# Early norm inputs, squares on other engines, a narrower index-key weight and a wider table row in a hybrid decoder layer

## The chip, the cores and the metric

The kernel runs on one core of one Trainium2 chip. The metric is device time in microseconds (us) of one execution; lower is better. An execution's time is a little longer than the span of its trace, which runs from the first to the last instruction.

Five engines work side by side, each through its own list of instructions in order: PE (TensorE; PE rows are matmuls, PEld rows are their weight loads), DVE (VectorE), ACT (ScalarE), POOL (GpSimd) and SP (SyncE, which issues most DMAs). They wait for each other by semaphores.

## The reference

One decoder layer over 256 tokens of 1024 features. What bears on the change is cut out here:

```python
def rms_norm(x, g):
    xf = x.astype(jnp.float32)
    y = xf * lax.rsqrt(jnp.mean(xf * xf, axis=-1, keepdims=True) + EPS)
    return (y * g.astype(jnp.float32)).astype(x.dtype)
...
def token_mixer(xn, w_in, conv_w, conv_b, w_r, b_r, w_i, b_i, lam, w_pa, w_pb, w_pc, w_o, rel_bias):
    proj = xn @ w_in
    (qa, ka, va, qb, kb, vb, qi, ki, wi, xc, yc, gates) = jnp.split(proj, IN_OFFSETS, axis=-1)
    y_a = moba_attention(..., rel_bias[:, :N_HEADS_A])
    y_b = dsa_attention(..., ki, wi, rel_bias[:, N_HEADS_A:])
    y_c = rg_lru(causal_depthwise_conv(xc, ...), ...) * jax.nn.gelu(yc)
    merged = g[:, :, 0] * (y_a @ w_pa) + g[:, :, 1] * (y_b @ w_pb) + g[:, :, 2] * (y_c @ w_pc)
    return merged @ w_o
...
    x = x + token_mixer(rms_norm(x, norm_mix_g[l]), ...)
    x = x + squared_relu_mlp(rms_norm(x, norm_mlp_g[l]), ...)
    return rms_norm(x, final_norm_g)
```

`ki` (64 columns) and `wi` (8 columns) are the index keys and index weights of the sparse branch. In both attention branches the logit of query t and key s gets a bias `rel_bias[bucket(t - s), head]`, 16 heads in all.

## The kernel before

Every product is kept near float32 accuracy by splitting each operand into a high part (a rounded copy, made by ACT) and a low part (the rest, made by DVE with one subtraction), and by three matmul passes: high by high, high by low, low by high. A weight tile is two halves of 128 x 1024 floats. A half arrives by DMA in a `raw` buffer (5 of them), ACT writes its `hi` (L133) and DVE its `lo` (L134); there are 6 `hi` and 6 `lo` buffers. PE then spends 24 matmuls of 256 columns on a half (L198). A `raw` buffer is free, and SP may issue the next load into it, once its `lo` is done.

The first stage is written out by hand (`manual_schedule`: on ACT, DVE, POOL and PE its instructions stand in the order of the code). The transposed input arrives in four slices of 128 x 512 in `xr`, each with a quarter of weight tile 0 behind it. For a slice ACT writes two pieces of `xnh` (L291), DVE two of `xnl` (L293), then both split the weight slice, and PE runs 12 matmuls into `ps_qi0` (L300). The norm's scale 1/rms is left out at this point and multiplied in later. It comes from squares of the slices (`sq`, L307 on POOL, L309 on ACT for the last), three sums (L311) and a fold (`sqs`, L312) on POOL, a ones-matmul over partitions (`ps_r`, L316), `v` (L322, DVE), the power -1/2 (`y`, L323, POOL), four small DVE instructions (L325 to L328, giving `r1`) and two diagonal matrices (`dg`, L332), which PE spreads over all partitions (L340). PE meanwhile runs weight tile 1 (second half of the index queries, `ps_qi1`), the index keys and weights (`ps_kw`, L336) and the next tiles. `first_queries` (L274 to L278) turns `ps_qi0` and `ps_qi1` into operands; it is one ACT and five DVE instructions.

POOL also runs a chain of some 20 instructions of four columns (L462 to L474) for the recurrence's decay, each waiting for the last.

PSUM for projections is three accumulators (`acc_tile`). `ps_qi0`, `ps_xc0` and `ps_yc0` lie in the same one, in the built programs of before and after; `ps_yc0` can start when DVE has read `ps_xc0` (`xp`, L398).

The bias: a table of 33 x 16 numbers times a one-hot matrix gives 16 rows of 384 (`psr`, L371), DVE copies them to `rrow` (L373), and one DMA from POOL's queue (L375) writes each row 32 times to DRAM (`toep`), 512 runs of 383 floats. Eight loads of each attention branch read from there (L383). DVE adds the first of these at L587.

After the first stage a scheduler that works on the code's priorities sets the order on each engine; `order` rows below show what came out.

Of the kernel before, what the change touches and what calls it, by code (L numbers as in the profile page):

```python
# [20 lines left out]
F32 = mybir.dt.float32  # L21
# [17 lines left out]
NB = 383  # L39
TOEP_W = 384  # L40
COPIES = 32
TOEP_H = COPIES * 386


C_GMIX, C_GMLP, C_CW, C_CB, C_BR, C_BI, C_LAM = 0, 8, 16, 32, 36, 40, 44
# [13 lines left out]
def layer(ctx, tc, x, xf, wts, kiwi, small, wri, rel_bias, onehot, gfin, out):  # L59
# [16 lines left out]
    def f(ap):  # L76
        return ap.bitcast(F32)
# [136 lines left out]
    xnl = const.tile([P, 8, S], F32R, name="xnl", tag="xnl")  # L214
    xn = (xnh, xnl)

    xr = [wp.tile([P, 1024], F32, tag="raw", name=f"xr{j}", bufs=RAW_BUFS) for j in range(2)]
    w0 = [tuple(wp.tile([P, 1024], dt, tag=p, name=f"{p}0_{j}", bufs=n)
                for p, dt, n in (("raw", F32, RAW_BUFS), ("hi", F32R, HL_BUFS), ("lo", F32R, HL_BUFS)))
          for j in range(2)]  # L220
# [2 lines left out]
        nc.sync.dma_start(xr[i // 2][:, d], xf[:, s])  # L223
        nc.sync.dma_start(w0[i // 2][0][:, d], wts[0, :, s])
    loaded[1] = load(1)
    kw = big("kw")
    nc.sync.dma_start(kw, kiwi)
    loaded[2] = load(2)
    next_tile[0] = 2
# [50 lines left out]
    def split_tile(i, j):  # L280
        raw, hi, lo = loaded[i][j]
        split(hi, lo, raw)

    with tc.manual_schedule(engines=ENGINES):
        pv = ps_q[0].rearrange("p (c t) -> p c t", c=2)
        for i in range(4):
            xi = xr[i // 2].rearrange("p (k t) -> p k t", k=4)
            d = slice(i % 2 * 512, (i % 2 + 1) * 512)
            raw, hi, lo = (z[:, d] for z in w0[i // 2])
            for k in (2 * i, 2 * i + 1):  # L290
                nc.scalar.activation(xnh[:, k, :], xi[:, k % 4, :], AF.Copy, scale=sp[:, C_GMIX + k:C_GMIX + k + 1])  # L291
            for k in (2 * i, 2 * i + 1):
                nc.vector.scalar_tensor_tensor(xnl[:, k, :], xi[:, k % 4, :], sp[:, C_GMIX + k:C_GMIX + k + 1],  # L293
                                               f(xnh[:, k, :]), op0=ALU.mult, op1=ALU.subtract)
            split(hi, lo, raw)
            for n, (a, b) in enumerate(((0, 0), (0, 1), (1, 0))):
                for k in (2 * i, 2 * i + 1):
                    ww = w0[i // 2][1 + a].rearrange("p (k c) -> p k c", k=4)
                    for c in range(2):
                        nc.tensor.matmul(pv[:, c, :], ww[:, k % 4, c * P:(c + 1) * P], xn[b][:, k, :],  # L300
                                         start=(i == 0 and n == 0 and k == 0 and c == 0),
                                         stop=(i == 3 and n == 2 and k == 7 and c == 1))

        for i in range(4):
            xi = xr[i // 2][:, i % 2 * 512:(i % 2 + 1) * 512]
            if i < 3:
                nc.gpsimd.tensor_mul(sq[i], xi, xi)  # L307
            else:
                nc.scalar.activation(sq[i], xi, AF.Square)  # L309
            if i > 0:  # L310
                nc.gpsimd.tensor_add(sq[0], sq[0], sq[i])  # L311
        nc.gpsimd.tensor_add(sqs, sq[0][:, :S], sq[0][:, S:])  # L312
        split_tile(1, 0)
        fmajor(ps_q[1], [z[1:] for z in loaded[1]], xn, cs=(0,))
        for t in range(2):
            nc.tensor.matmul(ps_r[:, S + t:S + t + 1], sqs[:, t * P:(t + 1) * P], ones[:, :1], start=True, stop=True)  # L316
        split_tile(1, 1)
        fmajor(ps_q[1], [z[1:] for z in loaded[1]], xn, cs=(1,))
        first_queries(0)

        v, y, b = (sm.tile([P, 2], F32, name=f"{n}_n1", tag=n) for n in ("v", "y", "b"))
        nc.vector.tensor_scalar(v, ps_r[:, S:S + 2], 1.0 / DM, EPS, op0=ALU.mult, op1=ALU.add)  # L322
        nc.gpsimd.tensor_tensor(y, v, mhalf.to_broadcast([P, 2]), op=ALU.pow)  # L323
        split(kwh, kwl, kw.rearrange("p (k c) -> p k c", c=P))
        nc.vector.tensor_mul(b, y, y)  # L325
        nc.vector.tensor_mul(b, b, v)
        nc.vector.tensor_scalar(b, b, -0.5, 1.5, op0=ALU.mult, op1=ALU.add)
# [37 lines left out]
    psr = att_tile("psr", "t")  # L365
    ohr = tmp("ohr", 384, F32R)[:33]
    nc.scalar.activation(ohr, oh, AF.Copy)
    tabs = [tiny_.tile([33, 16], F32R, name=f"tab{p}") for p in "hl"]
    split(*tabs, tab)
    for m in range(2):  # L370
        nc.tensor.matmul(psr[:16, :384], tabs[m], ohr, start=(m == 0), stop=(m == 1))  # L371
    rrow = tmp("rrow", 384)[:16]
    nc.vector.tensor_copy(rrow, psr[:16, :384])  # L373
    toep = dpool.tile([16, TOEP_H], F32, name="toep")
    nc.gpsimd.dma_start(  # L375
        bass.AP(tensor=toep.tensor, offset=toep.offset, ap=[[TOEP_H, 16], [TOEP_W + 1, COPIES], [1, NB]]),
        rrow[:, None, :NB].to_broadcast([16, COPIES, NB]))

    def load_bias(h0, name):

# [573 lines left out]
```

## Time and profile before

| | before |
|---|---|
| median of 3 runs | 457.63 us (457.39 to 457.86) |
| the profiled execution | 457.67 us |
| its span | 455.9 us |
| PE busy | 443.4 us (97%) |
| DVE busy | 341.4 us (75%) |
| ACT busy | 264.7 us (58%) |
| POOL busy | 30.9 us (7%) |
| mean granted TensorE clock | 0.997 of full speed |

The page's slices (40 of them, 11.4 us each, a digit is the busy share in tenths) show where each engine works:

```profile
PE   6899899999999999999999999999999999999994
DVE  7979899999989999975788686655555555555545
ACT  6467668775459698675634457444444444444463
POOL 6920110000010100000000000000000000000000
DMA  7869967524765453555555654556555555565202
```

The busy share of an engine is an average over stages with different limits; a stage is read from its own rows. Two rows of a timeline, a start and a later start on the same engine, give the time between them. PE's busy time includes the draining of its pipeline, so that a gap is longer between the weight loads (PEld) than PE's own idle time says.

### The profile page before, as it was taken

The numbers are of one execution on the slowest core, as the hardware profiler recorded it, in microseconds if no ns is written. First come the engines' busy times: TensorE is split into PE (matmuls) and PEld (weight loads), VectorE is DVE, ScalarE is ACT, GpSimd is POOL, SyncE is SP. The second block draws the span as 40 slices with busy tenths as digits, with TensorE's granted clock in tenths as the row PEclk, the third lists the DMA queues.
The fourth block names the chain that finished last, engine by engine and source line by source line (L and its number), as shares of the span: only waits on it lengthen the run. The fifth ranks groups of instructions, "written<-read, shape, count | busy, mean of one in ns | idle before, by whom it ended". The sixth has DMA issues, their size and how long they took to land.

```text
span 455.9 us, 7378 instructions
## 1 busy us (share of the span) xinstructions
PE 443.4 (97%) x2738; PEld 398.6 (87%) x2738; DVE 341.4 (75%) x652; ACT 264.7 (58%) x439; POOL 30.9 (7%) x66
## 2 busy tenths in 40 slices
PE   6899899999999999999999999999999999999994
PEld 6899889989988888888888889999999999999984
DVE  7979899999989999975788686655555555555545
ACT  6467668775459698675634457444444444444463
POOL 6920110000010100000000000000000000000000
PEclk9999999999999999999999999999999999999998
DMA  7869967524765453555555654556555555565202
GB/s 261 280 241 216 316 221 237 197 95 136 252 211 187 136 185 98 185 185 184 182 170 188 223 163 149 184 192 191 188 189 191 188 188 186 190 191 185 88 0 93
DMA packets 23840, 83.65 MB, mean 184 GB/s; under 512 B 2987, under 2 KB 3020, under 8 KB 23804
## 3 DMA queue, kind: packets, MB, share of 16 engines
q1 hardware_dynamic: 22700, 80.28, 53.4%
q0 software_dynamic: 960, 2.88, 3.0%
q8 instruction: 21, 0.34, 0.3%
q14 instruction: 15, 0.12, 0.1%
q10 hardware_dynamic: 144, 0.02, 0.0%
HBM read 81.34 MB, written 1.83 MB: 182 GB/s over the span
## 4 chain that ended last, share of the span: by engine, by line
PE 88%; DMA 3%; DVE 3%; POOL 3%; issue 2%; ACT 1%; SPq 0%; DVEq 0%; ACTq 0%
PE ps_up L198 20%; PE pd L775 19%; PE ps_g L208 14%; PE ps_p L208 7%; PE po L208 5%; DMA raw<-wts 3%; PE ps_qa L198 3%; PE ps_qb L198 3%; PE ps_kb L198 3%; PE ps_ka L198 3%; PE ps_vb L208 2%; PE ps_va L208 2%; DVE lo L134 1%; PE ps_yc L198 1%; POOL sp L468 1%
## 5 line engine op out<-in xcount | busy, mean ns | idle before, releaser
L134 DVE TENSOR_TENSOR lo<-raw,hi 128x1024 fp32r<-128x1024 f32 (+1 forms) x146 | 178.8, 1236 | 81.5 <-ACT hi L133 81.0
L133 ACT ACTIVATE hi<-raw 128x1024 fp32r<-128x1024 f32 (+1 forms) x146 | 150.0, 1044 | 123.8 <-PE pd L775 42.8
L775 PE MATMUL pd<-hi,hh 128*128 128x512 f32 (+1 forms) x128 | 49.4, 387 | 0.0
L775 PE MATMUL pd<-hi,hl 128*128 128x512 f32 (+1 forms) x128 | 49.4, 387 | 0.0
L775 PE MATMUL pd<-lo,hh 128*128 128x512 f32 (+1 forms) x128 | 49.2, 386 | 0.0
L198 PE MATMUL ps_up<-x2h,hi 128*128 128x256 f32 x256 | 36.6, 283 | 0.0
L198 PE MATMUL ps_up<-x2h,lo 128*128 128x256 f32 x256 | 36.6, 283 | 0.0
L198 PE MATMUL ps_up<-x2l,hi 128*128 128x256 f32 x256 | 36.6, 283 | 0.0
L198 PEld LDWEIGHTS ps_up<-x2h,hi 128*128 128x128 f32 x256 | 34.0, 191 | 1.0
L198 PEld LDWEIGHTS ps_up<-x2h,lo 128*128 128x128 f32 x256 | 33.3, 192 | 0.0
L198 PEld LDWEIGHTS ps_up<-x2l,hi 128*128 128x128 f32 x256 | 33.3, 192 | 0.0
L208 PE MATMUL ps_g<-hi,xnh 128*128 128x512 f32 x96 | 30.4, 391 | 0.0
L208 PE MATMUL ps_g<-lo,xnh 128*128 128x512 f32 x96 | 30.3, 393 | 0.0
L208 PE MATMUL ps_g<-hi,xnl 128*128 128x512 f32 x96 | 30.2, 392 | 0.0
L775 PEld LDWEIGHTS pd<-lo,hh 128*128 128x128 f32 x128 | 24.0, 188 | 4.9
L775 PEld LDWEIGHTS pd<-hi,hh 128*128 128x128 f32 x128 | 24.1, 188 | 4.5
L775 PEld LDWEIGHTS pd<-hi,hl 128*128 128x128 f32 x128 | 24.1, 188 | 4.4
L208 PEld LDWEIGHTS ps_g<-hi,xnh 128*128 128x128 f32 x96 | 17.9, 188 | 3.4
L208 PEld LDWEIGHTS ps_g<-lo,xnh 128*128 128x128 f32 x96 | 17.8, 188 | 3.6
L208 PEld LDWEIGHTS ps_g<-hi,xnl 128*128 128x128 f32 x96 | 17.8, 188 | 3.4
L167 POOL TENSOR_TENSOR ssq_n<-q_n 128x1 f32<-128x1 f32 x2 | 0.4, 194 | 279.4 <-ACT scr_n L165 279.4
L663 ACT ACTIVATE g<-ps_g,rh 128x512 f32<-128x512 f32 x12 | 8.2, 682 | 9.4 <-PE ps_g L208 9.4
(370 smaller groups left out, 823.0 us busy)
## 6 DMA issues: line engine op xcount, KB each, us to landing
raw<-wts SPq DMA_DIRECT2D x142, 512.0 KB, 4.9
xr<-xf SPq DMA_DIRECT2D x4, 256.0 KB, 6.2
raw<-wts SPq DMA_DIRECT2D x4, 256.0 KB, 5.8
x<-x SPq DMA_DIRECT2D x2, 512.0 KB, 4.1
biasb<-toep POOLq DMA_DIRECT2D x8, 128.0 KB, 7.0
biasa<-toep POOLq DMA_DIRECT2D x8, 128.0 KB, 2.8
out<-o SPq DMA_DIRECT2D x2, 512.0 KB, 2.6
toep<-rrow POOLq DMA_DIRECT2D x1, 766.0 KB, 10.3
```

The source lines that it names most:

```text
L133: nc.scalar.activation(hi, raw, AF.Copy)
L134: nc.vector.tensor_sub(lo, raw, f(hi))
L167: nc.gpsimd.tensor_add(ssq, q[:, 0:1], q[:, 1:2])
L198: nc.tensor.matmul(pv[:, c, :], ww[a][:, k, :], xx[b][:, k, :], start=(n == 0 and k == 0 and (c == 0 or not part)), stop=(n == 2 and k == ...
L208: nc.tensor.matmul(ps, xx[b][:, k0 + k, d], ww[a][:, k, :], start=(first and n == 0 and k == 0), stop=(last and n == 2 and k == nk - 1))
L468: nc.gpsimd.tensor_mul(sp8, sp8, sq_)
L663: nc.scalar.activation(g[:, t, :], ps, AF.Tanh, scale=rh[:, t:t + 1])
L775: nc.tensor.matmul(ps, hid[g][b][:, c, d], w_down[g][c][a][:, s], start=(g == (NG - LAG if o else 0) and c == 0 and m == 0), stop=(g == NG ...
```

## The change

Four edits are made together.

- The transposed input's slices land in the two tiles `xt` that later hold the token-major x, and not in two `raw` buffers. All five `raw` buffers are then free for weights. Weight tile 1's second half is now loaded ahead of `kw`.
- All four squares are on ACT, behind the `hi` of both halves of tile 1. The three sums and the fold are on DVE. The ones-matmul stands behind both halves of tile 1, not between them. `v` is read, and POOL's power asked for, ahead of `first_queries(0)`.
- `kiwi` is loaded without its 56 zero columns (288 KB for 512 KB), split as 8 x 72 columns, and POOL sets the remaining columns of `kwh` and `kwl` to zero. The spreading of `dg` stands behind all of `ps_kw`.
- The bias table has each head's column 8 times, so that `psr` and `rrow` have 128 rows, and the DMA to `toep` takes 4 copies from each of 128 partitions, not 32 from each of 16. The number of runs and of bytes stays.

```diff
--- before.py
+++ after.py
@@ -27,6 +27,7 @@
 DRAM = bass.MemoryType.DRAM
 
 P = 128
+KW = 72
 S = 256
 DM = 1024
 NH = 8
@@ -39,7 +40,7 @@
 NB = 383
 TOEP_W = 384
 COPIES = 32
-TOEP_H = COPIES * 386
+TOEP_H = COPIES * (TOEP_W + 1)
 
 
 C_GMIX, C_GMLP, C_CW, C_CB, C_BR, C_BI, C_LAM = 0, 8, 16, 32, 36, 40, 44
@@ -214,7 +215,8 @@
     xnl = const.tile([P, 8, S], F32R, name="xnl", tag="xnl")
     xn = (xnh, xnl)
 
-    xr = [wp.tile([P, 1024], F32, tag="raw", name=f"xr{j}", bufs=RAW_BUFS) for j in range(2)]
+
+    xr = xt
     w0 = [tuple(wp.tile([P, 1024], dt, tag=p, name=f"{p}0_{j}", bufs=n)
                 for p, dt, n in (("raw", F32, RAW_BUFS), ("hi", F32R, HL_BUFS), ("lo", F32R, HL_BUFS)))
           for j in range(2)]
@@ -223,7 +225,7 @@
         nc.sync.dma_start(xr[i // 2][:, d], xf[:, s])
         nc.sync.dma_start(w0[i // 2][0][:, d], wts[0, :, s])
     loaded[1] = load(1)
-    kw = big("kw")
+    kw = big("kw")[:, :8 * KW]
     nc.sync.dma_start(kw, kiwi)
     loaded[2] = load(2)
     next_tile[0] = 2
@@ -260,6 +262,8 @@
     qiq = big("qiq", F32R).rearrange("p (c j t) -> p c j t", c=4, j=2)
     qil = tmp("qil", 512, F32R).rearrange("p (c t) -> p c t", c=4)
     kwh, kwl = (z.rearrange("p (k c) -> p k c", c=P) for z in (big("kwh", F32R), big("kwl", F32R)))
+    for z in (kwh, kwl):
+        nc.gpsimd.memset(f(z[:, :, KW:]), 0.0)
     rr = const.tile([P, S], F32, name="rr")
     r1 = tiny_.tile([P, 2], F32, name="r1")
     ki2 = tmp("ki2", S)
@@ -300,28 +304,24 @@
                         nc.tensor.matmul(pv[:, c, :], ww[:, k % 4, c * P:(c + 1) * P], xn[b][:, k, :],
                                          start=(i == 0 and n == 0 and k == 0 and c == 0),
                                          stop=(i == 3 and n == 2 and k == 7 and c == 1))
+        split_tile(1, 0)
+        split_tile(1, 1)
 
         for i in range(4):
-            xi = xr[i // 2][:, i % 2 * 512:(i % 2 + 1) * 512]
-            if i < 3:
-                nc.gpsimd.tensor_mul(sq[i], xi, xi)
-            else:
-                nc.scalar.activation(sq[i], xi, AF.Square)
+            nc.scalar.activation(sq[i], xr[i // 2][:, i % 2 * 512:(i % 2 + 1) * 512], AF.Square)
             if i > 0:
-                nc.gpsimd.tensor_add(sq[0], sq[0], sq[i])
-        nc.gpsimd.tensor_add(sqs, sq[0][:, :S], sq[0][:, S:])
-        split_tile(1, 0)
+                nc.vector.tensor_add(sq[0], sq[0], sq[i])
+        nc.vector.tensor_add(sqs, sq[0][:, :S], sq[0][:, S:])
         fmajor(ps_q[1], [z[1:] for z in loaded[1]], xn, cs=(0,))
+        fmajor(ps_q[1], [z[1:] for z in loaded[1]], xn, cs=(1,))
         for t in range(2):
             nc.tensor.matmul(ps_r[:, S + t:S + t + 1], sqs[:, t * P:(t + 1) * P], ones[:, :1], start=True, stop=True)
-        split_tile(1, 1)
-        fmajor(ps_q[1], [z[1:] for z in loaded[1]], xn, cs=(1,))
-        first_queries(0)
+        split(kwh[:, :, :KW], kwl[:, :, :KW], kw.rearrange("p (k c) -> p k c", c=KW))
 
         v, y, b = (sm.tile([P, 2], F32, name=f"{n}_n1", tag=n) for n in ("v", "y", "b"))
         nc.vector.tensor_scalar(v, ps_r[:, S:S + 2], 1.0 / DM, EPS, op0=ALU.mult, op1=ALU.add)
         nc.gpsimd.tensor_tensor(y, v, mhalf.to_broadcast([P, 2]), op=ALU.pow)
-        split(kwh, kwl, kw.rearrange("p (k c) -> p k c", c=P))
+        first_queries(0)
         nc.vector.tensor_mul(b, y, y)
         nc.vector.tensor_mul(b, b, v)
         nc.vector.tensor_scalar(b, b, -0.5, 1.5, op0=ALU.mult, op1=ALU.add)
@@ -335,9 +335,8 @@
             for k in range(8):
                 nc.tensor.matmul(ps_kw[:, :S], (kwh, kwl)[a][:, k, :], xn[b][:, k, :], start=(n == 0 and k == 0),
                                  stop=(n == 2 and k == 7))
-            if n == 1:
-                for t in range(2):
-                    nc.tensor.matmul(ps_r[:, t * P:(t + 1) * P], ones, dg[t], start=True, stop=True)
+        for t in range(2):
+            nc.tensor.matmul(ps_r[:, t * P:(t + 1) * P], ones, dg[t], start=True, stop=True)
         first_queries(1)
         split_tile(2, 1)
         nc.scalar.activation(rr, ps_r[:, :S], AF.Copy)
@@ -365,16 +364,19 @@
     psr = att_tile("psr", "t")
     ohr = tmp("ohr", 384, F32R)[:33]
     nc.scalar.activation(ohr, oh, AF.Copy)
-    tabs = [tiny_.tile([33, 16], F32R, name=f"tab{p}") for p in "hl"]
-    split(*tabs, tab)
+
+    tabs = [tmp(f"tab{p}", P, F32R)[:33].rearrange("p (h c) -> p h c", c=8) for p in "hl"]
+    split(*tabs, tab[:, :, None].to_broadcast([33, 16, 8]))
     for m in range(2):
-        nc.tensor.matmul(psr[:16, :384], tabs[m], ohr, start=(m == 0), stop=(m == 1))
-    rrow = tmp("rrow", 384)[:16]
-    nc.vector.tensor_copy(rrow, psr[:16, :384])
+        nc.tensor.matmul(psr[:, :384], tabs[m].rearrange("p h c -> p (h c)"), ohr, start=(m == 0), stop=(m == 1))
+    rrow = tmp("rrow", 384)
+    nc.vector.tensor_copy(rrow, psr[:, :384])
     toep = dpool.tile([16, TOEP_H], F32, name="toep")
+    n = COPIES // 8
     nc.gpsimd.dma_start(
-        bass.AP(tensor=toep.tensor, offset=toep.offset, ap=[[TOEP_H, 16], [TOEP_W + 1, COPIES], [1, NB]]),
-        rrow[:, None, :NB].to_broadcast([16, COPIES, NB]))
+        bass.AP(tensor=toep.tensor, offset=toep.offset,
+                ap=[[n * (TOEP_W + 1), P], [TOEP_W + 1, n], [1, NB]]),
+        rrow[:, None, :NB].to_broadcast([P, n, NB]))
 
     def load_bias(h0, name):
 
@@ -935,7 +937,7 @@
         "xf": _fm(i["x"][0].T),
         "wts": _weight_tiles(w_in, i["w_pa"][0], i["w_pb"][0], i["w_pc"][0], i["w_o"][0],
                              i["w_up"][0], i["w_down"][0]),
-        "kiwi": _fm(np.concatenate([w_in[:, 3584:3656], np.zeros((DM, 56), w_in.dtype)], axis=1)),
+        "kiwi": _fm(w_in[:, 3584:3656]),
         "small": small,
         "wri": np.concatenate([_blockdiag(i["w_r"][0]), _blockdiag(i["w_i"][0])], axis=1),
         "rel_bias": i["rel_bias"],
```

PE around the ones-matmul and the index keys, from the second half of tile 1 on. Before (`hi_1_146` and `lo_1_147` are that half, `ps_xc_598` is `ps_xc0`, tile 2):

```order
L316 MATMUL ps_r<-ones,sqs 128x1 x2
L198 MATMUL ps_qi_168<-xnh,hi_1_146 128x256 x8
L198 MATMUL ps_qi_168<-xnl,hi_1_146 128x256 x8
L198 MATMUL ps_qi_168<-xnh,lo_1_147 128x256 x8
L336 MATMUL ps_kw<-xnh,kwh 128x256 x8
L336 MATMUL ps_kw<-xnl,kwh 128x256 x8
L198 MATMUL ps_xc_598<-xnh,hi_0_152 128x256 x8
L198 MATMUL ps_xc_598<-xnl,hi_0_152 128x256 x8
L340 MATMUL ps_r<-dg_338,ones 128x128
L340 MATMUL ps_r<-dg_339,ones 128x128
L336 MATMUL ps_kw<-xnh,kwl 128x256 x8
L198 MATMUL ps_xc_598<-xnh,lo_0_153 128x256 x8
```

The same place after:

```order
L199 MATMUL ps_qi_166<-xnh,hi_1_144 128x256 x8
L199 MATMUL ps_qi_166<-xnl,hi_1_144 128x256 x8
L199 MATMUL ps_qi_166<-xnh,lo_1_145 128x256 x8
L318 MATMUL ps_r<-ones,sqs 128x1 x2
L336 MATMUL ps_kw<-xnh,kwh 128x256 x8
L336 MATMUL ps_kw<-xnl,kwh 128x256 x8
L336 MATMUL ps_kw<-xnh,kwl 128x256 x8
L199 MATMUL ps_xc_598<-xnh,hi_0_150 128x256 x8
L199 MATMUL ps_xc_598<-xnl,hi_0_150 128x256 x8
L339 MATMUL ps_r<-dg_338,ones 128x128
L339 MATMUL ps_r<-dg_339,ones 128x128
L199 MATMUL ps_xc_598<-xnh,lo_0_151 128x256 x8
```

The ones-matmul has gone behind 24 matmuls, and the third pass of `ps_kw` ahead of 16 matmuls of `ps_xc0` and of the spreading of `dg`; from the low pass of `ps_xc0` on both have done the same work.

DVE from tile 1's low parts to the small instructions of the norm. Before:

```order
L134 TENSOR_TENSOR lo_0_143<-raw_0_140,hi_0_142 128x1024
L134 TENSOR_TENSOR lo_1_147<-raw_1_144,hi_1_146 128x1024
L275 TENSOR_TENSOR qil<-ps_qi_167,qi 128x256
L277 CAST qiq<-qi 64x2x128
L278 TENSOR_TENSOR qiq<-ps_qi_167,qi 64x2x128
L277 CAST qiq<-qi 64x2x128
L278 TENSOR_TENSOR qiq<-ps_qi_167,qi 64x2x128
L322 TENSOR_SCALAR v_n_327<-ps_r 128x2
L134 TENSOR_TENSOR tabl<-tab,tabh 33x16
L134 TENSOR_TENSOR kwl<-kw,kwh 128x1024
L325 TENSOR_TENSOR b_n_329<-y_n_328 128x2
```

The same place after (without the two low parts, which stand ahead of it):

```order
L313 TENSOR_TENSOR sq_179<-sq_179,sq_180 128x512
L313 TENSOR_TENSOR sq_179<-sq_179,sq_181 128x512
L313 TENSOR_TENSOR sq_179<-sq_179,sq_182 128x512
L314 TENSOR_TENSOR sqs<-sq_179 128x256
L135 TENSOR_TENSOR kwl<-kw,kwh 128x8x72
L322 TENSOR_SCALAR v_n_323<-ps_r 128x2
L279 TENSOR_TENSOR qil<-ps_qi_165,qi 128x256
L281 CAST qiq<-qi 64x2x128
L282 TENSOR_TENSOR qiq<-ps_qi_165,qi 64x2x128
L281 CAST qiq<-qi 64x2x128
L282 TENSOR_TENSOR qiq<-ps_qi_165,qi 64x2x128
L325 TENSOR_TENSOR b_n_325<-y_n_324 128x2
```

Four instructions have come in ahead of `kwl`, and `first_queries(0)` now stands behind `v`.

DVE up to the reading of `ps_xc0`. Before (`lo_0_806` and `lo_1_810` are the halves of tile 4):

```order
L134 TENSOR_TENSOR lo_0_806<-raw_0_803,hi_0_805 128x1024
L346 TENSOR_TENSOR ki_177<-ps_kw,rr 64x256 x2
L482 TENSOR_TENSOR wrl<-wrt,wrh 128x1024
L373 COPY rrow<-psr 16x384
L398 TENSOR_TENSOR xp<-ps_xc_598,rr 128x2x256
L134 TENSOR_TENSOR lo_1_810<-raw_1_807,hi_1_809 128x1024
```

The same place after:

```order
L135 TENSOR_TENSOR lo_0_806<-raw_0_803,hi_0_805 128x1024
L484 TENSOR_TENSOR wrl<-wrt,wrh 128x1024
L345 TENSOR_TENSOR ki_177<-ps_kw,rr 64x256 x2
L135 TENSOR_TENSOR lo_1_810<-raw_1_807,hi_1_809 128x1024
L400 TENSOR_TENSOR xp<-ps_xc_598,rr 128x2x256
```

A low part stands ahead of `xp` now, and the copy to `rrow` has gone further back, behind `wi` (L392) and the low parts of tile 7; the matmuls of `psr` have gone back with it, out of the middle of tile 2 into tile 5 (`ps_yc0` and `ps_yc1`).

## Rows read from the trace of the kernel before

**Rows 1.** Windows. Columns: engines' busy us (instructions), clock, DMA share, GB/s

```profile
60.00:440.00 380.00, 380.00 (x2297) 339.86 (x2296) 281.69 (x541) 224.65 (x369) 4.74 (x10) 1.00 0.54 175
```

**Rows 2.** Waits of PE's weight loads. Columns: us in total, times, longest us

```profile
PEld ps_qi L300 <- DVE lo L134: 3.7, 4, 1.1
...
PEld l_i L413 <- ACT rl L424: 1.7, 1, 1.7
```

**Rows 3.** Timeline, PE's weight loads. Columns: start us, us, engine, line

```profile
16.42 1.03 PEld L198 LDWEIGHTS ps_qi<-xnh,hi 128*128 128x128 f32 x8
...
19.30 0.54 PEld L316 LDWEIGHTS ps_r<-ones,sqs 128*128 128x128 f32 x4
...
22.62 1.03 PEld L336 LDWEIGHTS ps_kw<-xnh,kwh 128*128 128x128 f32 x8
...
27.86 1.03 PEld L198 LDWEIGHTS ps_xc<-xnh,lo 128*128 128x128 f32 x8
...
28.82 0.55 PEld L198 LDWEIGHTS ps_xc<-xnh,hi 128*128 128x128 f32 x4
...
30.42 1.03 PEld L198 LDWEIGHTS ps_xc<-xnl,hi 128*128 128x128 f32 x8
...
38.10 1.03 PEld L198 LDWEIGHTS ps_yc<-xnh,hi 128*128 128x128 f32 x8
```

**Rows 4.** DVE instructions by form. Columns: count, busy us, mean ns, idle before

```profile
L134 DVE TENSOR_TENSOR lo<-raw,hi 128x512 fp32r<-128x512 f32 x4 | 6.6, 1643 | 0.0
...
L763 DVE TENSOR_TENSOR hl<-r,hh 128x512 fp32r<-128x512 f32 x16 | 11.1, 691 | 0.5
...
L497 DVE SCALAR_TENSOR_TENSOR xc<-xp,sp,xc 128x256 f32<-128x256 f32 x12 | 5.1, 477 | 0.0
```

**Rows 5.** POOL's squares by form

```profile
L307 POOL TENSOR_TENSOR sq<-xr 128x512 f32<-128x512 f32 x3 | 3.5, 1155 | 2.4 <-DMA xr<-xf 2.4
```

**Rows 6.** Timeline, a small POOL instruction beside one of DVE

```profile
20.74 1.28 POOL L468 TENSOR_TENSOR sp<-sp,sq__557 128x4 f32<-128x4 f32 x1
...
20.74 1.21 DVE L134 TENSOR_TENSOR kwl<-kw,kwh 128x1024 fp32r<-128x1024 f32 x1
```

**Rows 7.** Timeline: ACT's hi of the last weight slice; SP's issue of kw

```profile
5.74 0.67 SPq L227 DMA_DIRECT2D kw<-kiwi  x1
...
10.98 0.62 ACT L133 ACTIVATE hi<-raw 128x512 fp32r<-128x512 f32 x1
```

**Rows 8.** DMA issues, whole span. Columns: count, KB each, median us to landing

```profile
kw<-kiwi SPq DMA_DIRECT2D x1, 512.0 KB, 7.5
...
raw<-wts SPq DMA_DIRECT2D x142, 512.0 KB, 4.9
...
toep<-rrow POOLq DMA_DIRECT2D x1, 766.0 KB, 10.3
...
out<-o SPq DMA_DIRECT2D x2, 512.0 KB, 2.6
```

**Rows 9.** Timeline of ACT, a hi that waits for its weights

```profile
48.56 1.06 ACT L133 ACTIVATE hi<-raw 128x1024 fp32r<-128x1024 f32 x1 [4.10 <-DMA raw<-wts]
```

**Rows 10.** Timeline, DVE and POOL around the norm, and the reading of ps_xc0

```profile
18.65 0.41 DVE L275 TENSOR_TENSOR qil<-ps_qi,qi 128x256 fp32r<-128x256 f32 x1
...
20.46 0.16 DVE L322 TENSOR_SCALAR v_n<-ps_r 128x2 f32<-128x2 f32 x1
...
24.33 0.73 POOL L323 TENSOR_TENSOR y_n<-v_n,mhalf 128x2 f32<-128x2 f32 x1
...
25.09 0.16 DVE L325 TENSOR_TENSOR b_n<-y_n 128x2 f32<-128x2 f32 x1 [3.13 <-POOL y_n L323]
...
36.56 0.67 DVE L398 TENSOR_TENSOR xp<-ps_xc,rr 128x512 f32<-128x512 f32 x1
```

**Rows 11.** The chain that ended last, one piece. Columns: start us, us, what

```profile
38.38 10.09 DMA raw<-wts
```

**Rows 12.** A reader of biasb. Columns: count, ns min/median/max, first, last start

```profile
L587 DVE TENSOR_TENSOR b2b<-biasb,score x8: 407/546/686, 129.9 to 155.3; 128x256 f32<-128x256 f32 x4, 128x512 f32<-128x512 f32 x4
```


## Prediction

> **What bounds the kernel now.** I read the windows first. From 60 to 440 us PE is busy in all 380 us [rows 1]. There the time is the sum of the matmuls, and the change alters none of them in number or columns. Only the start and the end can gain, and the edits lie in the start. So the second view is what PE waits for: in the whole trace its weight loads wait 3.7 us in total, four times, for a `lo` of the first tile, and once 1.7 us for ACT's `rl` [rows 2]. The third view, the timeline, puts dates on PE's course through the start [rows 3]: tile 1 begins at 16.42 us, the ones-matmul stands at 19.30, `ps_kw` begins at 22.62, the low pass of `ps_xc0` at 27.86, `ps_yc0` at 38.10. What PE wins at one of these points and does not lose later comes off the end.
>
> **Part 1: the squares leave POOL.** The four `lo` of the first tile took 1643 ns each, and 16 subtractions of the same 128 x 512 on the same engine took 691 [rows 4]. Beside the slow ones POOL ran multiplies of 1155 ns over the same slices [rows 5]. That the two engines keep each other waiting shows best in a pair: a POOL instruction of four columns took 1.28 us while DVE's `kwl` took 1.21, both from 20.74 on [rows 6]. With POOL's wide work gone I price `lo` at 0.69 us and an `xnl` piece at 0.48, as another instruction of that shape and kind takes [rows 4].
>
> ACT's work on the four slices is fed by DMAs whose order does not change, so its last `hi` still ends at 10.98 + 0.62 = 11.60 us [rows 7]. DVE's `lo` of that slice ends at 12.3 us if only it is left by then, at 11.60 + 2 x 0.48 + 0.69 = 13.25 if both `xnl` pieces are left too; these wait only for `xnh`, which ACT writes ahead of that `hi`, so I take 12.6. Half a tile is 24 matmuls and took 19.30 - 16.42 = 2.88 us, 0.12 each [rows 3]; four more matmuls and a hop of 0.1 bring PE to tile 1 at 13.2 us, 3.2 earlier (2.6 to 3.5).
>
> [...] In rows 6 it is the small one that waits, and DVE's 1.21 us for 1024 columns is no longer than two of 691 ns. [...]
>
> **Part 2: can everything behind it keep up?** PE's tile 1 would run from 13.2 to 13.2 + 2 x 2.88 = 19.0 us.
> - Weights: the second half now takes `kw`'s place in the queue, issued at 5.74 us [rows 7]; `kw`, of the same size, landed 7.5 us after its issue [rows 8], so at 13.2. ACT's `hi` of a half takes 1.06 us [rows 9], the two end by about 13 and 14.3, DVE's `lo` at 1.21 each [rows 6] by 15.5; PE needs the last of them at 18.0.
> - Squares: four on ACT at the 0.62 us of a copy of that shape [rows 7] end at 16.8. Three sums at 0.69 and a fold of half the width follow them; the last sum and the fold end at 17.9. PE wants them at 19.0: 1.1 us to spare. `kwh` and `kwl`, 576 columns for 1024, follow at 17.5 and 18.7, wanted at 19.4 and 21.3. POOL's two fills of zeros, 448 columns each, are not in the trace; by its multiply of 512 columns they take at most 1.2 us each [rows 5], and they stand in the middle of its small chain, long before 19.4. Cost on the path: nothing, as long as this second holds.
> - The ones-matmul takes 22.62 - 19.30 - 2.88 = 0.44 us [rows 3] and brings `ps_kw` to 19.4, still 3.2 earlier.
> - The new wait: DVE's `v` stands ahead of `first_queries(0)` and waits for that matmul, until 19.5. Behind it are the five query instructions, 20.46 - 18.65 = 1.8 us [rows 10]; they end at 21.5. `ps_xc0` uses their accumulator and starts after `ps_kw`, at 19.4 + 2.88 = 22.3: 0.8 to spare. POOL's power (0.73 us [rows 10]) is done at 20.6, under the queries. So `r1`'s first instruction starts at 21.6; before it was 25.09, after 3.1 us of waiting [rows 10], since POOL came to the power only behind squares and chain. `dg` and the `lo` of tile 2 follow by about 24.1; PE reaches the low pass of `ps_xc0` at 22.3 + 16 x 0.12 + 0.44 = 24.7, before 27.86.
>
> **Part 3: up to `ps_yc0`.** PE took 38.10 - 27.86 = 10.24 us there. In it are `psr`'s two matmuls, which now come later: 8 matmuls from 28.82 to 30.42 took 1.60 us for 0.96, so they cost 0.64 [rows 3]. PE would be at `ps_yc0` at 24.7 + 9.6 = 34.3. Its accumulator must be read by `xp` first. From `r1`'s first instruction to the end of `xp` DVE took 36.56 + 0.67 - 25.09 = 12.14 us [rows 10], all of it work. Now the copy to `rrow` is gone from it (384 columns, some 0.5 us) and a `lo` of 1.21 has come in: 12.8, so `xp` ends at 21.6 + 12.8 = 34.4, and PE waits about 0.3 us (0 to 0.9). `psr`'s matmuls return later between others, for 0.2 to 0.6; with the 0.64 saved here I book 0.2 us of gain (0 to 0.4).
>
> **Part 4: the second gap.** PE lost 1.7 us to `rl` [rows 2]. The `rl` stood on ACT behind a `hi` that waited 4.10 us for weights, until 48.56 [rows 9]; these had been issued at 38.38 and took 10.09 us [rows 11] where 4.9 are usual [rows 8]. Between lay the write of `toep`, 10.3 us for 766 KB [rows 8]. Those weights go into the buffer that the second `lo` of tile 4 frees; in part 3 it ends at 34.4 - 0.7 = 33.7, and no `toep` is under way then. For `toep` now starts further back: between `xp` and the copy to `rrow` DVE has six `lo` of 1.21 [rows 6], six instructions as the 0.48 one of rows 4 and some ten smaller ones, in all about 13.5 us, so near 48. The gap goes, 1.7 us. The bias is first added at 129.9 us [rows 12], so a later `toep` harms no reader. It can harm later weights. How long the write takes from 128 partitions the trace does not show. The bounds are 10.3 us, since runs and bytes stay, and 3.9, the 2.6 us of `out`, from 128 partitions, scaled to its bytes [rows 8]. A short write costs PE nothing, a long one up to the same 1.7 us; I take 0.4, nearer the short end, since the partitions are those of `out`.
>
> [...]
>
> **Sum**, against the profiled execution's 457.67 us, 0.04 from the median: - 3.2 + 0.3 - 0.2 - 1.7 + 0.4 = - 4.4, so 453.3 us. By the bounds of the terms this case runs from 452.0 to 454.6.
>
> **Rivals.**
> - *The second gap comes back.* `toep` takes its 10 us at the new place, weights land late, an `rl` stands behind them on ACT again. For it: ACT's order after still mixes `hi` and `rl` there. Against: the partitions. Then only the start's gain is left: 457.67 - 3.0 = 454.7 (to 455.6 with term 1 at its low end).
> - *The weight stream is the bound.* PE asks earlier than the DMAs can deliver, and what is won at 13 us is lost by 60. For it: the 10.09 us landing. Against: PE waited for no weights but there. The gain is then the 224 KB less of `kiwi`: at most 4.9 x 224 / 512 = 2.1 us with loads one after another [rows 8], near 0.7 since several are under way at once: 457.
> - *Slower: the sums hold PE up.* The `lo` were slow for another reason than POOL, and stay at 1.64; so are the sums. DVE leaves tile 1's low parts where it did, at 18.65 [rows 10], the sums and the fold take 3 x 1.64 + 0.9 = 5.8, to 24.5, and PE stands at the ones-matmul from 16.42 + 5.76 = 22.2 on, all of `ps_kw` and tile 2 behind it: 2.3 us, and the second gap stays: 460.0. It decides once a sum takes over 1.4 us. Against it: 691 ns, 16 times.
>
> **How the numbers follow.** Forecast 0.62, second gap 0.23, weight stream 0.09, slower 0.06. A difference below 0.2% (0.9 us) cannot be told from none. Faster: the first two, 0.85; same: the third, 0.09; slower 0.06. The range 452.0 to 455.7 takes in the first two with their bounds.
>
> **What would show it.** In the profile after: `lo` of 128 x 512 near 0.7 us; tile 1 on PE at 13.2, `ps_kw` at 19.4, low pass of `ps_xc0` at 24.7, `ps_yc0` near 34.5; no idle of PE at the ones-matmul; `toep` near 48 us and under 5 us long; no wait for `rl` over 0.5. I am wrong if `lo` stays above 1 us, if PE idles at the ones-matmul or before `ps_yc0` by over 1 us, or if PE has new gaps between 45 and 100 us.

## The result and the profile after

| | median, us | runs | range |
|---|---|---|---|
| before | 457.51 | 4 | 457.26 to 457.86 |
| after | 454.70 | 4 | 454.64 to 456.36 |

The ratio is 0.9947 (95% interval 0.9923 to 0.9970): 2.8 us faster, where 4.4 us were forecast. The profiled execution is the one of 456.36 us (span 454.6); the three others had spans of 452.9.

PE's weight loads in the start, the timeline of after (start us, us, engine, line, operation; in brackets the wait ahead and what ended it). It answers to [rows 3]:

```profile
13.69 1.03 PEld L199 LDWEIGHTS ps_qi<-xnh,hi 128*128 128x128 f32 x8
...
19.45 0.54 PEld L318 LDWEIGHTS ps_r<-ones,sqs 128*128 128x128 f32 x4
19.90 1.02 PEld L336 LDWEIGHTS ps_kw<-xnh,kwh 128*128 128x128 f32 x8
...
25.14 1.02 PEld L199 LDWEIGHTS ps_xc<-xnh,lo 128*128 128x128 f32 x8
...
35.02 1.01 PEld L199 LDWEIGHTS ps_yc<-xnh,hi 128*128 128x128 f32 x8 [0.22 <-issue]
...
41.23 0.18 PEld L371 LDWEIGHTS psr<-ohr,tabh 33*128 33x128 f32 x1 [1.72 <-ACT tabh L134]
41.60 0.41 PEld L199 LDWEIGHTS ps_yc<-xnl,hi 128*128 128x128 f32 x3 [0.18 <-issue]
```

Tile 1 starts 2.73 us earlier, `ps_yc0` 3.08 earlier (35.02 for 38.10). Then comes something new: PE stands 1.72 us before `psr`. The waits of its weight loads in the whole trace (us in total, times, longest) say the same, against [rows 2]:

```profile
PEld psr L371 <- ACT tabh L134: 1.7, 1, 1.7
PEld ps_qi L304 <- ACT hi L134: 1.1, 1, 1.1
...
PEld ps_ri L509 <- ACT xch L134: 0.3, 1, 0.3
PEld ps_vb L209 <- DVE vbl L559: 0.3, 1, 0.3
```

The four waits for `lo` and the one for `rl` are gone; `psr`, `ps_ri` and `ps_vb` have come in. DVE by form, first 20 us (count, busy us, mean ns), with the slow `lo` of [rows 4] cured:

```profile
L135 DVE TENSOR_TENSOR lo<-raw,hi 128x512 fp32r<-128x512 f32 x4 | 2.8, 691 | 0.3 <-ACT hi L134 0.2
...
L313 DVE TENSOR_TENSOR sq<-sq,sq 128x512 f32<-128x512 f32 x3 | 2.1, 689 | 0.2
```

Why `tabh` is late shows in ACT's timeline. Three `hi` in a row wait for their weights, and `tabh`, 0.29 us of work on values that were there long before, stands behind them:

```profile
30.55 1.06 ACT L134 ACTIVATE hi<-raw 128x1024 fp32r<-128x1024 f32 x1 [4.71 <-DMA raw<-wts]
33.50 1.06 ACT L134 ACTIVATE hi<-raw 128x1024 fp32r<-128x1024 f32 x1 [1.89 <-DMA raw<-wts]
36.25 1.06 ACT L134 ACTIVATE hi<-raw 128x1024 fp32r<-128x1024 f32 x1 [1.68 <-DMA raw<-wts]
...
40.89 0.29 ACT L134 ACTIVATE tabh<-tab 33x128 fp32r<-33x128 f32 x1
```

The DMA issues of the whole span (count, KB, median us to landing), against [rows 8]:

```profile
raw<-wts SPq DMA_DIRECT2D x142, 512.0 KB, 4.8
...
toep<-rrow POOLq DMA_DIRECT2D x1, 766.0 KB, 8.3
```

From 60 to 440 us PE is busy in all 380 us, as in [rows 1]. All of the difference lies in the start: PE comes to `ps_va`, behind it, at 90.52 us for 92.06 in the kernel before, 1.54 earlier, and the spans differ by 1.3.

### The profile page after: what moved, and what is told of

The parts are those of the page before. It is cut to its first block, busy times and chain, and to the rows that moved or that the text cites. A ratio compares the mean times of both kernels' runs of the same rounds, so it can differ in the third digit from the quotient of the medians.

```text
span 454.6 us, 7382 instructions
## 1 busy us (share of the span) xinstructions
PE 445.2 (98%) x2738; PEld 400.6 (88%) x2738; DVE 338.0 (74%) x656; ACT 267.0 (59%) x442; POOL 24.6 (5%) x61
## 4 chain that ended last, share of the span: by engine, by line
PE 92%; DMA 2%; DVE 2%; ACT 2%; issue 1%; ACTq 0%; DVEq 0%
PE ps_up L199 20%; PE pd L777 19%; PE ps_g L209 14%; PE ps_p L209 7%; PE po L209 5%; PE ps_qa L199 3%; PE ps_qb L199 3%; PE ps_ka L199 3%; PE ps_kb L199 3%; PE ps_vb L209 2%; PE ps_va L209 2%; PE ps_qi L304 2%; DMA raw<-wts 2%; PE ps_yc L199 2%; PE ps_qi L199 1%; DMA sp<-small 1%
## 5 line engine op out<-in xcount | busy, mean ns | idle before, releaser
L135 DVE TENSOR_TENSOR lo<-raw,hi 128x1024 fp32r<-128x1024 f32 (+1 forms) x146 | 174.3, 1208 | 82.8 <-ACT hi L134 82.0
```

## The experiments

Ten runs, each kernel timed beside the kernel before on the same chip. The first four, then the next four, then the last two were run together; the kernel before took 457.58, 457.68 and 457.70 us. All medians:

| kernel | median, us (range) | ratio to before | interval |
|---|---|---|---|
| e1: after, again | 455.01 (454.66 to 455.84) | 0.9944 | 0.9932 to 0.9957 |
| e2: after, `tabs` in a buffer of its own | 453.29 (452.95 to 453.53) | 0.9902 | 0.9889 to 0.9915 |
| e3: after, table of 16 rows | 456.74 (454.89 to 459.11) | 0.9979 | 0.9961 to 0.9996 |
| e4: after, squares on POOL | 456.77 (456.60 to 457.62) | 0.9984 | 0.9976 to 0.9993 |
| e5: before, table of 128 rows, shared buffers | 456.27 (456.17 to 456.45) | 0.9969 | 0.9958 to 0.9980 |
| e6: before, table of 128 rows, own buffer | 456.39 (455.92 to 456.68) | 0.9968 | 0.9956 to 0.9981 |
| e7: e2, `kiwi` with zero columns | 453.52 (453.27 to 454.91) | 0.9913 | 0.9899 to 0.9927 |
| e8: e2, 12 matmuls of zeros | 453.48 (453.23 to 453.84) | 0.9909 | 0.9894 to 0.9925 |
| e9: e2, early x in `raw` buffers | 454.53 (454.32 to 454.98) | 0.9928 | 0.9915 to 0.9941 |
| e10: e2, again | 453.78 (453.01 to 453.91) | 0.9909 | 0.9893 to 0.9924 |

### The same kernel once more (e1)

> The changed kernel once more, for a second profile. In the first profile the matmuls of tile 0 took 0.21 us each until 10.3 us and 0.12 behind that, its span was 454.6 us, and three other executions had 452.9. Theory A (clock): those three ran tile 0 at 0.12 a matmul; a profile at 0.12 has tile 1 at about 13.3 us (its weights bound it) instead of 13.69, so A explains 0.4 us of the 1.7, unless the later wait of psr for tabh (1.7 us) shrinks too. Theory B (the wait): the executions differ in the wait of psr, and a span of 452.9 has psr waiting under 0.3 us. Time: 454.7 (454.5 to 456.4).

Measured: 455.01 us, span 453.1. The same places of PE's timeline, in e1:

```profile
39.81 0.18 PEld L371 LDWEIGHTS psr<-ohr,tabh 33*128 33x128 f32 x1
40.18 0.41 PEld L199 LDWEIGHTS ps_yc<-xnl,hi 128*128 128x128 f32 x3 [0.18 <-issue]
...
45.13 0.18 PEld L371 LDWEIGHTS psr<-ohr,tabl 33*128 33x128 f32 x1
45.50 0.42 PEld L199 LDWEIGHTS ps_yc<-xnh,lo 128*128 128x128 f32 x3 [0.19 <-issue]
...
58.07 0.19 PEld L509 LDWEIGHTS ps_ri<-xch,wrh 128*128 128x128 f32 x1 [0.34 <-ACT xch L134]
58.55 0.30 PEld L209 LDWEIGHTS ps_vb<-hi,xnh 128*128 128x128 f32 x2 [0.30 <-DVE vbl L559]
```

Here `tabh` ran at 38.36, 2.5 us earlier than in the first trace, and PE did not wait for it. So the two traced executions differ by the wait for `tabh`, as theory B had it: 1.72 us of wait, 1.5 of span. It comes or stays away with the `hi` ahead of `tabh` (the last of three that wait for weights ran at 36.25 in after, at 33.72 in e1). The three other executions of after, 1.7 us shorter than the first, have no trace; their spans (452.9) are near that of e1. The 1.7 us still missing from the forecast in e1 are not that wait.

### `tabs` in a buffer of its own (e2 and e10)

```diff
-    tabs = [tmp(f"tab{p}", P, F32R)[:33].rearrange("p (h c) -> p h c", c=8) for p in "hl"]
+    tq = queries("tabs", 3)
+    tabs = [tq[:33, i].rearrange("p (h c) -> p h c", c=8) for i in range(2)]
```

> The changed kernel with tabh and tabl in a buffer of their own (an attention buffer that is idle then), not in the four shared buffers of 256 columns; everything else as in the change. In the built order psr's matmuls stand in tile 2 again and rrow ahead of xp. Theory A (late place): PE's wait for tabh goes, toep is written from about 33 us in 8 us or less; 1.3 to 1.7 us less than the changed kernel, about 453.2. Theory B (weights bound): weights issued near 33 us land late behind toep as before the change, the wait comes back at rl; the time of the changed kernel, 454.7.

> The kernel after with `tabs` in a buffer of its own, once more, beside the run with x in the `raw` buffers. Theory A (the shared buffer of `tabs` alone cost 1.7 us): 453.3 us again (453.0 to 453.7), ratio to the kernel before 0.990, no wait of PE over 0.5 us after the first tile. Rival B (453.29 was a lucky set of runs): above 454 us.

Measured: 453.29 and 453.78 us, the second 0.1 above what I had given it and below the 454 of rival B. This version beats both kernels. Only the buffer of the two small tiles is edited against e1, and with it the order on the engines changes: in e2's timeline of PE both `psr` matmuls stand at 27.22, one behind the other, and ACT writes `tabs` at 18.11:

```profile
27.22 0.29 PEld L372 LDWEIGHTS psr<-ohr,tabs 33*128 33x128 f32 x2
27.76 1.01 PEld L199 LDWEIGHTS ps_xc<-xnl,hi 128*128 128x128 f32 x8 [0.25 <-issue]
```

The waits of its weight loads in the whole trace are only these:

```profile
PEld ps_qi L304 <- ACT hi L134: 1.1, 1, 1.1
PEld warm L131 <- DVE zero L129: 1.1, 1, 1.1
PEld ps_xc L199 <- issue: 0.3, 1, 0.3
```

The new order cost e1 1.53 us by `ps_va` (timelines of before, e1 and e2, in this order):

```profile
92.06 0.31 PEld L208 LDWEIGHTS ps_va<-hi,xnh 128*128 128x128 f32 x2
89.10 0.31 PEld L209 LDWEIGHTS ps_va<-hi,xnh 128*128 128x128 f32 x2
87.57 0.31 PEld L209 LDWEIGHTS ps_va<-hi,xnh 128*128 128x128 f32 x2
```

At `ps_yc0` e1 was still 0.23 us ahead (35.19 for 35.42), so that it lost 1.76 behind it. The rows name two parts of that: the two `psr` matmuls, paid singly (39.81 to 40.18 and 45.13 to 45.50, 0.37 each), and the waits of `ps_ri` and `ps_vb`, 0.34 and 0.30. The remaining 0.4 us stand in no wait that the profile lists; they stay open.

### The table of 16 rows in the kernel after (e3)

```diff
-    split(*tabs, tab[:, :, None].to_broadcast([33, 16, 8]))
+    tabs = [tiny_.tile([33, 16], F32R, name=f"tab{p}") for p in "hl"]
+    split(*tabs, tab)
...
-    rrow = tmp("rrow", 384)
+    rrow = tmp("rrow", 384)[:16]
...
-        rrow[:, None, :NB].to_broadcast([P, n, NB]))
+        rrow[:, None, :NB].to_broadcast([16, COPIES, NB]))
```

The lines left out here put back the table of before in the same way: `TOEP_H`, the two matmuls and the target of the DMA.

> The changed kernel with the table of before: 16 rows, 32 copies from each of 16 partitions, tabs in their old buffers; psr's matmuls stand early here too. Against the run with 128 partitions and own buffers it tells what the partitions are worth. [...] Theory B (runs and bytes, not partitions, set the time of toep): as the run with own buffers, within 0.3 us.

Measured: 456.74 us, 0.8 less than before, 2.0 above the 454.70 of after and 3.45 above e2, in which `psr` stands just as early (theory B falls). So the table is worth 3.45 us where the start is gained. PE came to `ps_yc0` at 35.80 instead of 38.10 and gave the gain back at `rl` (waits of weight loads, then PE's timeline there):

```profile
PEld l_i L413 <- ACT rl L424: 2.8, 1, 2.8
```

```profile
48.83 0.29 PEld L413 LDWEIGHTS l_i<-keysh,qi 128*128 128x128 f32 x1 [2.81 <-ACT rl L424]
```

`toep` was issued at 34.3, and the weights asked for at 35.17 took as long as in [rows 11] (the chain of waits: start us, us, what):

```profile
35.17 10.24 DMA raw<-wts
```

`toep` itself took 10.6 (the DMA issues of e3):

```profile
toep<-rrow POOLq DMA_DIRECT2D x1, 766.0 KB, 10.6
```

These weights landed at 45.41, 3.1 us earlier than in the kernel before (38.38 + 10.09 = 48.47). But in e3 the two `xc` and one more `hi` stand on ACT between the late `hi` and the `rl`, so that `rl` ran only 1.1 us earlier (48.42 for 49.52), while PE had come 2.3 earlier to `ps_yc0`: 2.81 us of wait for 1.73. Behind it PE ran slowly:

```profile
48.99 0.34 PEld L413 LDWEIGHTS l_i<-keysl,qi 128*128 128x128 f32 x1
49.21 0.34 PEld L413 LDWEIGHTS l_i<-keysh,qil 128*128 128x128 f32 x1
...
50.50 1.18 PEld L199 LDWEIGHTS ps_yc<-xnh,hi 128*128 128x128 f32 x4
...
53.29 0.19 PEld L413 LDWEIGHTS l_i<-keysh,qi 128*128 128x128 f32 x1
```

The granted clock was 0.50 from 49 to 51 us, 0.62 and 0.67 in the microsecond ahead of that and behind it, and 1.00 elsewhere between 44 and 58 (0.97 in the mean of the first 60 us); behind the shorter wait of the kernel before, 1.73 us, it stayed at 1.00. From 48.83 to 53.29 PE took 4.46 us for what e2, at a granted clock of 1.00, did in 3.23 (45.58 to 48.81). So 2.30 gained less 1.08 of longer wait less 1.23 of clock is nothing: this execution comes to `ps_va` at 92.06, as the kernel before does, and took 457.74 us.

The other executions have no trace. The twelve spread from 454.89 to 459.11 us, and on the whole the longer ones have the lower mean granted clock: 0.998 and 0.999 in the two shortest (454.89 and 455.05), 0.989 in the two longest (458.81 and 459.11). By this trace the 0.8 us by which the median lies below the kernel before are what is left of the start's gain after a longer wait and a fall of the clock; in the two shortest executions 2.5 to 2.7 are left. How wait and clock share the loss in the other executions stays open.

### The table alone in the kernel before (e5 and e6)

The edit is that of the table in the change, with `tabs` in the shared buffers (e5) or as in e2 (e6).

> The kernel before with the table on 128 partitions alone, as the change writes it: `tabs` in the buffers that other work shares, so that `psr`'s first matmul stands behind `ps_yc0`'s first 12. Theory A (a `toep` from 128 partitions lands in 7 to 8.5 us and lets the weights behind it come in time, so the 1.7 us at `rl` goes; but the late place of `psr` costs 1.5 us of its own, for PE waits there for ACT's `tabh` behind a `hi` that waits for weights): 457.4 us (456.8 to 457.8), the wait for `rl` below 0.5, a wait of 1 us or more at `psr`. Rival B (the late place costs nothing by itself; PE only waited there because it came 3 us earlier than before): 455.8 us, no wait at `psr`. Rival C (the gap at `rl` goes only because the whole start is earlier, not because of the partitions): 457.6 us with the wait for `rl` still over 1 us.

> The kernel before with the table on 128 partitions, `tabs` in a buffer that is free from the start, so that `psr`'s matmuls keep their early place. Theory A: the wait of 1.7 us at `rl` goes and nothing takes its place, 455.8 us (455.3 to 456.4), `toep` 7 to 8.5 us long. Rival C (the partitions alone don't bring the weights in time): the wait at `rl` stays over 1 us and the time within 0.5 us of the kernel before, 457.6.

Measured: 456.27 and 456.39 us, no difference between them; e5 lies below theory A's 457.4 and above rival B's 455.8. The wait for `rl` is 0.4 in e6 and gone in e5. In e6 `toep` stands as early as in the kernel before (issued at 37.1 for 36.9) and lands in 7.9 us for 10.3. The edit is the wider table alone (with it the 16 rows of `toep` lie 32 numbers closer in DRAM, which no run separates): it takes 1.3 of the gap's 1.7 us away (rival C falls), and the kernel gains 1.3 us. e5 shows that my theory of the late place was too simple: there it costs nothing, as rival B said. PE comes to `psr` at 39.11, and ACT had written `tabh` at 37.48:

```profile
39.11 0.18 PEld L371 LDWEIGHTS psr<-ohr,tabh 33*128 33x128 f32 x1
```

So the late place showed a price only where PE comes earlier: it was at `ps_yc0` at 37.47 in e5, at 35.02 in after.

### Squares on POOL again (e4)

```diff
-            nc.scalar.activation(sq[i], xr[i // 2][:, i % 2 * 512:(i % 2 + 1) * 512], AF.Square)
+            xi = xr[i // 2][:, i % 2 * 512:(i % 2 + 1) * 512]
+            nc.gpsimd.tensor_mul(sq[i], xi, xi)
             if i > 0:
-                nc.vector.tensor_add(sq[0], sq[0], sq[i])
-        nc.vector.tensor_add(sqs, sq[0][:, :S], sq[0][:, S:])
+                nc.gpsimd.tensor_add(sq[0], sq[0], sq[i])
+        nc.gpsimd.tensor_add(sqs, sq[0][:, :S], sq[0][:, S:])
```

> The changed kernel with the four squares, the sums and the fold on POOL, in the changed order; all else as in the change. Theory A (POOL and DVE keep each other waiting): the 128x512 lo take 1.5 us or more, tile 1 begins on PE at about 16.4 us, 2.7 to 3.2 later, and the time is 457 to 458. Theory B (the start was gained by x in its own tiles and earlier weights): lo near 0.7 or slow without effect, tile 1 at 13.7, the time of the changed kernel within 0.5.

Measured: 456.77 us, 1.8 more than e1 and a little under the 457 to 458 of theory A. DVE by form, first 20 us of e4:

```profile
L135 DVE TENSOR_TENSOR lo<-raw,hi 128x512 fp32r<-128x512 f32 x4 | 5.5, 1365 | 0.0
L297 DVE SCALAR_TENSOR_TENSOR xnl<-x,sp,xnh 128x256 fp32r<-128x256 f32 x8 | 5.4, 718 | 2.4 <-ACT xnh L295 2.4
L135 DVE TENSOR_TENSOR lo<-raw,hi 128x1024 fp32r<-128x1024 f32 x2 | 3.4, 1760 | 0.0
```

Each of these DVE instructions, beside POOL's squares and sums, is slow again, the `lo` of 128 x 1024 too (1760 ns for 1226), and tile 1 starts at 16.04 us:

```profile
16.04 1.03 PEld L199 LDWEIGHTS ps_qi<-xnh,hi 128*128 128x128 f32 x8
```

The slices of x lie in `xt` and the weights are asked for early in e4 as well, so the start was not gained by these (theory B falls).

### Parts of the improved version (e7, e8, e9)

e7 puts the zero columns back into `kiwi`; e8 has `WARM = 12` for 9; e9 is e2 with this line:

```diff
-    xr = xt
+    xr = [wp.tile([P, 1024], F32, tag="raw", name=f"xr{j}", bufs=RAW_BUFS) for j in range(2)]
```

> The kernel after with `tabs` in a buffer of its own (453.3 us), and `kiwi` again with its 56 zero columns a tile: 512 KB for 288, `kwh` and `kwl` again of 1024 columns. Theory A (the weight stream has room; `kiwi` without zeros was worth next to nothing): 453.4 us (453.1 to 453.9), `ps_kw` at most 0.4 us later than 19.9. Rival B (PE asks as fast as the DMAs deliver, so 224 KB more cost their transfer time): 453.3 + 2.1 = 455.4 us with loads one after another, 454.0 with three under way at once, and PE waiting for `hi` or `lo` of weights between 20 and 60 us.

> The kernel after with `tabs` in a buffer of its own (453.3 us), and 12 instead of 9 matmuls of zeros ahead of the first tile, so that PE isn't idle from 5.3 to 6.1 us. Theory A (the idle 0.8 us let the clock fall, and so the first 20 matmuls of tile 0 took 0.21 us each for 0.12): they take 0.12, tile 1 begins at 13.3 instead of 13.7, 452.9 us. Rival B (the half rate has another reason): the matmuls behind the zeros still take 0.21, tile 1 begins at 13.7 or, as the zeros end at 6.7 instead of 5.3, some 0.6 later; 453.3 to 453.9 us.

> The kernel after with `tabs` in a buffer of its own (453.3 us), and the early x again in two of the five `raw` buffers, as in the kernel before. The second half of tile 1 then waits, on SP, for the first buffer of tile 0 to come free. Theory A (the loads have room): it is issued near 9.5 us instead of 5.5, lands by 15, its `lo` is done by 17, and PE wants it at 17.5; tile 1 runs without a gap and the time is 453.3 us (452.9 to 453.9). Rival B (the early second half is what lets PE run through tile 1): PE waits over 0.5 us for a `hi` or `lo` of tile 1 or 2 before 30 us, and the time is 454 to 455.3 us.

Measured: 453.52 (e7), 453.48 (e8) and 454.53 us (e9). Neither the zero columns nor the warm-up can be told from no change. e9 answers between its theories. Tile 1 ran without a gap, as theory A had it, and yet the time is 0.75 us above e10's, run beside it, and 1.24 above e2's. The price appears 27 us behind the end of tile 1, at `rl` (e9's timeline of PE):

```profile
46.85 0.19 PEld L416 LDWEIGHTS l_i<-keysh,qi 128*128 128x128 f32 x1 [1.12 <-ACT rl L427]
```

e7 had such a wait too, of 1.05 us in its profiled execution, and e8 one of 0.19. In the six traces with `toep` issued between 33.2 and 34.3 us this wait goes with the time that `toep` took: none at 7.8 and 8.1 us (e2, e10), 0.19 at 8.7 (e8), 1.12 at 9.4 (e9), 1.05 at 9.6 (e7) and 2.81 at 10.6 (e3, 16 rows). Why one and the same write takes 7.8 us in one of them and 9.6 in another, and whether x in the `raw` buffers lengthens it in e9, no run shows.

## Why the prediction was right, and which term was mis-sized

**Part 1, right.** `lo` took 691 ns for the forecast 0.69, and e4 shows that POOL's squares and sums were the cause. Tile 1 began at 13.69 for 13.2. Most of the half us is not in the weights: in after, the first 16 matmuls of tile 0 took 0.21 us each instead of 0.12 (last section), and in e7 and e10, where they took 0.12, tile 1 began at 12.97 and 13.43, though PE waited for `hi` there. The term of 3.2 us measured 2.73 us. The traces give the size of the slowing: `lo` of 691 ns without POOL's squares and sums (after), 1365 beside them (e4). By what means POOL holds DVE up no run shows.

**Part 2, right.** No wait at the ones-matmul (19.45), `ps_kw` at 19.90, the low pass of `ps_xc0` at 25.14 for 24.7: the half us of tile 1, carried along. The sums took 689 ns each, so the slower rival falls. (By part 2's own dates, from 15.5 to 19.0 us for three sums and a fold, it would have decided once a sum took over 1.0 us, not 1.4.) The weight-stream rival, as I put it, falls too: e7's extra 224 KB cost nothing that can be told.

**Part 3, the step that failed.** The wait at `ps_yc0` was right: 0.22 us for a forecast 0.3. But I booked a gain of 0.2 us for `psr`, by pricing the return of its two matmuls at 0.2 to 0.6 us wherever they stand. That term was mis-sized. e1 against e2 shows the price of the move: 1.7 us in the medians, 1.5 in the course of PE. It is the change's edit of `tabs`, from tiles of their own to shared buffers, that moved it. Behind `ps_yc0` the two matmuls themselves cost 0.74 us, the waits that the new order brought at `ps_ri` and `ps_vb` 0.64, and 0.4 are not found. Nor did I ask when `tabh` would be ready at the new place. In the profiled execution of after PE waited 1.72 us for it; e1 had no such wait, so that the 1.7 us that e1 lacks do not hang on it. I had written that I would be wrong if PE had new gaps between 45 and 100 us. The large one stood at 41, and the two small ones, of 0.34 and 0.30 us, at 59.49 and 59.98.

**Part 4, right in effect, wrong in its size.** The 1.7 us at `rl` went. e6 shows that the wider write alone takes 1.3 of them away even at its old place, which the rival of a second gap had doubted. `toep` was issued at 49.20 (forecast near 48), but it landed in 8.3 us, and in 7.0 to 9.6 in the other runs with 128 rows, where I had expected under 5. It was 10.6 in e3. The short bound near which I had set my 0.4, an estimate of 3.9 us from `out` [rows 8], is about half of the 8.3. At its later place the write cost PE nothing: I booked 0.4 us, and no wait of PE's weight loads behind 49 us is put down to a DMA or a `hi` of weights. At the early place PE waited up to 1.1 us at `rl` with 128 rows too (e7 and e9).

**The sum** on PE's course in e1, against the kernel before: 35.19 - 38.10 = - 2.9 at `ps_yc0` (forecast - 3.6, for 34.5), - 1.7 at `rl` (forecast - 1.7), + 1.7 behind `ps_yc0` for the late `psr` (forecast: 0.2 to 0.6), together - 2.9; at `ps_va` it is 89.10 - 92.06 = - 2.96. With the one term taken away, e2 comes to 453.29 and e10 to 453.78: the forecast of 453.3 is near the time of the change without its move of `tabs`. That e2 meets it so closely is luck in part: it came to `ps_yc0` 2.7 us earlier (35.42), where the forecast's start is worth 3.1 with `psr` paid, and the 0.4 booked for `toep` made up for that. That 454.7 is also what the rival of a second gap gave is chance; that gap stayed away. Some bounds were added up wrongly: the terms' own bounds give 452.1 to 454.7, and 456.0 if `toep` costs its 1.7, for the 452.0 to 454.6 stated; the rival with term 1 at its low end gives 455.2, not 455.6.

**What I had not seen** is that the parts don't add in the medians. The table alone is worth 1.3 us (e6), the start alone 0.8 (0.2 to 1.8; e3), both 4.3 (e2). The kernel before stalls twice, at the slow `lo` of tile 0 and at `rl`, for weights that land late. Taking away the first alone lets PE arrive sooner at the second: in e3's trace it waits 2.81 us there instead of 1.73, and the granted clock falls to 0.50 behind the wait, for another 1.2. In the executions of e3 with the highest clock the start is worth 2.5 to 2.7, and then the parts come to 3.8 to 4.0, near the 4.3; so much of the missing sum may be the clock, which one trace alone shows.

## What to carry to other kernels

When a step is moved, price not only its own instructions but the date at which its inputs are ready at the new place: here a 0.29 us copy that slipped behind three `hi` that wait for weights held PE for 1.72 us in one execution and not in another. A tile that is taken from a shared ring for convenience can move its writer, and other work with it; look in the order for where it has gone. And test parts together as well as apart: removing the first of two stalls alone can show little of its worth, when PE then waits longer at the second and its clock falls there, as in e3's trace (2.81 us of wait for 1.73, a granted clock of 0.50 behind it). Where the executions of a kernel spread widely, as e3's did, look at the clock of each (0.989 to 0.999 there) before a cause is given.

## What the runs showed of the hardware

The profiled executions differ in the rate of PE's first matmuls, for one and the same kernel. In e2 (timeline of PE) the first 16 matmuls behind the matmuls of zeros took 0.21 us each:

```profile
1.07 4.21 PE L131 MATMUL warm<-zero 128*128 128x128 f32 x18 [1.07 <-DVE zero L129]
6.13 1.22 PE L304 MATMUL ps_qi<-xnh,hi 128*128 128x256 f32 x4 [0.84 <-ACT hi L134]
7.15 1.05 PE L304 MATMUL ps_qi<-xnl,hi 128*128 128x256 f32 x4
8.00 1.05 PE L304 MATMUL ps_qi<-xnh,lo 128*128 128x256 f32 x4
```

In e10, the same program, they took 0.12 from the first one on, after a longer idle time:

```profile
1.08 4.03 PE L131 MATMUL warm<-zero 128*128 128x128 f32 x18 [1.08 <-DVE zero L129]
6.50 0.74 PE L304 MATMUL ps_qi<-xnh,hi 128*128 128x256 f32 x4 [1.39 <-ACT hi L134]
7.07 0.64 PE L304 MATMUL ps_qi<-xnl,hi 128*128 128x256 f32 x4
```

In e5's trace this slow rate goes with a lower clock: the granted clock is 0.50 from 8 to 11 us (0.88 in the mean of the first 14), and four of these matmuls took 1.22 us for 0.74. But the granted clock of the first 14 us is 1.00 in the traces of e2 and e10; the windows of e2 (PE busy, instructions, clock, DMA share, GB/s):

```profile
0.00:14.00 14.00, 12.08 (x68) 1.00 0.82 290
```

So the clock row doesn't show it there, as it does in e5 and, with 0.50, behind e3's wait for `rl`. Nor are the idle 0.8 us ahead of tile 0 what explains it, as I had supposed for e8: in the trace of the kernel before the first four took 0.74 us and the next four 0.64, behind 0.82 us of idle time. What decides it stays open. It is worth little: tile 1 began 0.2 us later in e2 than in e10 (13.65 for 13.43), and the medians of e8 and e2 agree.
